# Two-layer decoder trunk on one core: first queries ahead of the first spread, attention interleaved eight steps later

## The chip, the core and the metric

The kernel runs on one core of one Trainium2 chip. The metric is the device time of one execution in microseconds (us). The core's engines work in parallel, each through its own queue in order: TensorE (PE in the profile, matmuls), VectorE (DVE), ScalarE (ACT), GpSimd (POOL) and SyncE (SP), which issues most of the DMAs. Sums of matmuls stand in PSUM, which has eight banks of 128x512 f32; everything else on the chip stands in SBUF.

## What is computed

Two layers on a sequence of 1024 tokens with 1024 channels. The first mixes by differential attention in 12 heads (two softmax maps for each head, the second weighted and subtracted), the second by causal pooling over windows. Both add a cross-attention over 256 memory tokens and a gate:

```
proj = rms_norm(h) @ W_in            # u (queries, keys, values), q_mem, gate
q, k = apply_rotary(q), apply_rotary(k)
s = q @ k.T * scale, causal          # 12 heads x 2 maps, 64 wide
p = softmax(s);  w = p[0] - lam * p[1]
o = rms_norm(w @ v) * (1 - lambda_init)
y = concat(o, memory_attention(q_mem)) * silu(gate)
h = h + y @ W_out
```

All matmuls keep f32 precision: each operand is split into a rounded part and a rest (`wh`, `wl` for weights, `hh`, `hl` for hidden values), and a product is three matmuls, lines 125 to 127.

## The kernel before

**Steps.** The whole projection work of the attention is a stream of small steps (`run_jobs`, line 168). A step is one of the 8 parts of a projection of one half of the sequence (512 tokens): three matmuls of 128x512. A projection has half 1 (tokens 512 to 1023) first and then half 0, 16 steps, and behind the last step of a half its evacuation is emitted (`query_evac`, `key_evac`, `value_evac`, `gate_evac`). The jobs are, in order, the values of head 0, then for each further head h its queries, its keys, the gate of head h-1 and its values, 64 steps for a head. `step(n)` takes n steps, `step_to(n)` steps up to a count n.

**Order.** TensorE's order is that in which the code emits; `attention_layer` (line 1334) writes it by hand. The other engines' queues are ordered by the compiler's scheduler, and each of them runs its queue strictly in sequence.

**Prologue** (line 337). x is loaded and scaled, the keys and queries of head 0 are projected for both halves outside the stream, and their evacuations are held back until the half's row scale is known. That scale comes from `row_means` (TensorE, `ms_h`, line 250), a Newton iteration on DVE (`rsxh`, `rsuh`, `rsyh`, lines 224 to 241) and `spread`: matmuls that copy the scale to all partitions (`bc_h`, line 530), an ACT copy to `rsb`, and on DVE the products of the rotation tables with it (lines 372 and 373). Then the held evacuations run: for a query or key, ACT copies four blocks of 32 partitions (`rot`, line 763), DVE and POOL multiply by the rotation tables (lines 764, 767) and add (768), and ACT and DVE split the result (`qa` and `qlo`, lines 783 to 785; `kb`, 802 and 803).

**Attention.** Head h's scores are made in blocks of 128 queries, i = 0 to 7. `scores` (line 834) emits the matmuls of both maps, adds the mask and takes the least on DVE (856), with two steps of the stream behind each set; then ACT takes two exponentials, one for each map (865). `combine` (871) takes the reciprocal (875) and the scaling (876) on DVE, the second map's product on POOL (877) and the sum on DVE (880). The weights are used in ten groups (p, jj): `turn_weights` (884) transposes them on TensorE (`wt`, 902) and splits them, `apply_weights` (911) multiplies them by the values into `o`. Group k+1 is turned before group k is applied. Blocks 6, 7 and 4 of a head are scored ahead of its first group, blocks 2, 5 and 3 during groups 0, 1 and 2, and block 5 is first needed when group 4 (`wt` of p = 2) is turned. The last line of the loop, `self.step_to(60 + 64 * h + per_step * (g + 1))`, keeps the stream at 6.4 steps a group, 4.0 in the last head, where no queries, keys and values follow. `hooks` are the norms of finished outputs (`attend_post`, 929): a Newton iteration on 128x128 numbers on DVE (`rsya`, `rsua`) and a trip through DRAM. `turns` are transposes of values.

**Weights.** Each projection's weights are loaded by SP and split: ACT rounds them (`wh`, line 115), POOL subtracts (`wl`, line 118).

## Time and profile before

| | us |
|---|---|
| median of 3 runs | 1843.71 |
| lowest and highest | 1839.75, 1844.18 |
| the profiled execution | 1845.75 |
| its span, first to last instruction | 1844.0 |
| TensorE busy in it | 1742.3 (94%) |
| VectorE, ScalarE, GpSimd busy | 1351.8, 950.4, 658.8 |

The mean granted clock of TensorE is 0.98. The attention of head 0 begins at 86 us, and its ten groups take some 67 us a head; the first spread is at 40 us, the second at 50.7. A row of a timeline gives the start, the duration, the engine, the line, the operation, output<-inputs by the program's names without their numbers, and in brackets how long the engine had been idle and what released it. A row of a list of waits gives the total, the number and the longest.

### The profile page before, as it was taken

What the parts mean: (1) busy time and instruction counts of PE and PEld (TensorE: products, weight loads), DVE (VectorE), ACT (ScalarE), POOL (GpSimd) and SP (SyncE); (2) the same over time, 40 slices, a digit from 0 to 9 for tenths busy, and PEclk for the clock granted to TensorE, in tenths of its full rate; (3) what the DMA queues carried; (4) which work ended last, traced back from release to release, by engine and by line L of the source; (5) the groups of instructions that cost most, each with busy time, mean ns of one, the idle gap of its engine ahead of it and who ended that gap; (6) DMA issues with size and microseconds to landing.
All of it is one profiled execution on the core that took longest, in us unless ns stands there. A gap on an engine that the chain in (4) does not pass through costs nothing.

```text
span 1844.0 us, 24841 instructions
## 1 busy us (share of the span) xinstructions
PE 1742.3 (94%) x8478; PEld 1447.5 (79%) x8478; DVE 1351.8 (73%) x2705; ACT 950.4 (52%) x1764; POOL 658.8 (36%) x563
## 2 busy tenths in 40 slices
PE   6899999999999999999999998997999999979997
PEld 4778888888888888888787886875788777768886
DVE  7778888788888889886657768678876767754513
ACT  6667667567657657743246546454543332324422
POOL 4334344344444434343241243300133433413452
PEclk8999999999999999999999999998999999989998
DMA  5011111111111111011463777642312121156542
GB/s 185 23 35 47 46 46 58 46 35 58 47 46 47 47 52 52 35 64 64 155 211 110 267 263 260 218 175 91 106 61 89 63 80 67 54 177 194 172 151 95
DMA packets 81679, 188.68 MB, mean 102 GB/s; under 512 B 9200, under 2 KB 17104, under 8 KB 81552
## 3 DMA queue, kind: packets, MB, share of 16 engines
q1 hardware_dynamic: 79296, 183.08, 29.6%
q10 hardware_dynamic: 2160, 3.75, 0.6%
q8 instruction: 67, 1.10, 0.3%
q14 instruction: 60, 0.49, 0.1%
q0 software_dynamic: 96, 0.26, 0.0%
HBM read 155.29 MB, written 31.77 MB: 101 GB/s over the span
## 4 chain that ended last, share of the span: by engine, by line
PE 69%; DVE 17%; ACT 6%; DMA 5%; issue 3%; POOL 0%; SPq 0%; DVEq 0%; ACTq 0%; POOLq 0%
PE s L851 4%; PE o L925 3%; PE ob L127 3%; PE ob L125 3%; PE ob L126 3%; PE ga L125 3%; PE ga L126 3%; PE ga L127 3%; PE v L125 2%; PE v L127 2%; PE v L126 2%; PE wt L902 2%; DMA zf<-z 2%; ACT rotq L763 2%; PE q L125 2%
## 5 line engine op out<-in xcount | busy, mean ns | idle before, releaser
L865 ACT ACTIVATE e<-e,st 128x640 f32<-128x640 f32 (+4 forms) x192 | 148.2, 773 | 111.7 <-DVE st L856 110.5
L118 POOL TENSOR_TENSOR wl_o<-wf_o,wh_o 128x384 fp32r<-128x384 f32 x64 | 100.1, 1563 | 237.4 <-ACT wh_o L115 193.3
L877 POOL TENSOR_SCALAR e<-e,st 128x640 f32<-128x640 f32 (+4 forms) x96 | 76.3, 795 | 198.5 <-DVE st L876 115.2
L118 DVE TENSOR_TENSOR wl_o<-wf_o,wh_o 128x640 fp32r<-128x640 f32 x64 | 60.7, 948 | 107.7 <-ACT wh_o L115 98.7
L1575 DVE TENSOR_TENSOR zr<-zf,zr 128x512 fp32r<-128x512 f32 x132 | 108.2, 841 | 38.0 <-ACT zr L1574 37.6
L115 ACT CAST wh_o<-wf_o 128x1024 fp32r<-128x1024 f32 x64 | 67.2, 1050 | 117.0 <-PE ob L126 65.7
L905 ACT CAST wth<-wt 128x512 fp32r<-128x512 f32 (+2 forms) x168 | 72.5, 431 | 105.3 <-PE wt L902 74.0
L1574 ACT CAST zr<-zf 128x512 fp32r<-128x512 f32 x132 | 80.7, 619 | 83.6 <-DMA zf<-z 59.8
L856 DVE CUSTOM_DVE_ANT_0 e<-s,mask 128x512 f32<-128x512 f32 (+2 forms) x192 | 109.5, 581 | 10.5 <-PE s L851 8.9
L125 PE MATMUL ga<-hh,wh_ga 128*128 128x512 f32 x256 | 104.9, 410 | 3.8 <-DVE mqf L620 3.8
L127 PE MATMUL ob<-zr,wl_o 128*128 128x512 f32 x256 | 100.9, 394 | 6.1 <-DVE wl_o L118 6.1
L126 PE MATMUL ga<-hl,wh_ga 128*128 128x512 f32 x256 | 101.6, 397 | 0.0
L127 PE MATMUL ga<-hh,wl_ga 128*128 128x512 f32 x256 | 101.5, 396 | 0.0
L851 PE MATMUL s<-kb,qa 128*128 128x512 f32 (+2 forms) x288 | 98.4, 349 | 2.9 <-DVE kb L803 2.9
L126 PE MATMUL ob<-zr,wh_o 128*128 128x512 f32 x256 | 100.7, 393 | 0.4 <-DVE zr L1575 0.4
L125 PE MATMUL ob<-zr,wh_o 128*128 128x512 f32 x256 | 100.9, 394 | 0.0
L851 PE MATMUL s<-kb,qlo 128*128 128x512 f32 (+2 forms) x288 | 98.3, 349 | 0.0
L906 DVE TENSOR_TENSOR wtl<-wt,wth 128x512 fp32r<-128x512 f32 (+2 forms) x168 | 82.8, 493 | 7.8 <-ACT wth L905 6.6
L125 PE MATMUL k<-hh,wh_k 128*128 128x512 f32 x192 | 79.1, 412 | 9.1 <-ACT wh_k L115 9.1
L880 DVE SCALAR_TENSOR_TENSOR e<-e,st,e 128x640 f32<-128x640 f32 (+4 forms) x96 | 77.9, 811 | 9.7 <-POOL e L877 9.0
L902 PE MATMUL wt<-cst,e 128*128 128x128 f32 x432 | 69.2, 274 | 13.9 <-DVE e L880 11.4
L125 PE MATMUL v<-hh,wh_v 128*128 128x512 f32 x192 | 79.7, 415 | 0.0
(1225 smaller groups left out, 5653.2 us busy)
## 6 DMA issues: line engine op xcount, KB each, us to landing
zf<-z SPq DMA_DIRECT2D x132, 256.0 KB, 4.1
wf_o<-in_w_out SPq DMA_DIRECT2D x64, 512.0 KB, 3.6
wf_ga<-in_w_in SPq DMA_DIRECT2D x16, 512.0 KB
wf_q<-in_w_in SPq DMA_DIRECT2D x12, 512.0 KB, 3.2
wf_v<-in_w_in SPq DMA_DIRECT2D x12, 512.0 KB, 4.1
z<-rs SPq DMA_DIRECT2D x24, 256.0 KB, 3.3
z<-z SPq DMA_DIRECT2D x24, 256.0 KB, 2.0
wf_k<-in_w_in SPq DMA_DIRECT2D x11, 512.0 KB, 3.2
```

Source lines behind the costliest of these rows:

```text
L118: eng.tensor_tensor(wl[:, c], wf[:, c], wh[:, c].bitcast(F32), op=ALU.subtract)
L125: nc.tensor.matmul(out, sh, mh, start=first, stop=False, skip_group_check=more)
L126: nc.tensor.matmul(out, sh, ml, start=False, stop=False, skip_group_check=more)
L127: nc.tensor.matmul(out, sl, mh, start=False, stop=last, skip_group_check=more)
L851: nc.tensor.matmul(sc[m][:, w], q[half][part][:, m, qs], k[kh][:, m, w], start=(part == 0), stop=(part == 1),)
L856: nc.vector.tensor_tensor_reduce(out=es[m][:, lo:hi], in0=sc[m][:, : hi - lo], in1=self.mask[:, S - n + lo : S - n + hi], scale=1.0, scala ...
L865: nc.scalar.activation(es[m][:, :n], es[m][:, :n], AF.Exp, bias=least[m], scale=-1.0, accum_out=st[:, 2, m : m + 1],)
L880: nc.vector.scalar_tensor_tensor(es[0][:, :n], es[0][:, :n], st[:, 3, 0:1], es[1][:, :n], op0=ALU.mult, op1=ALU.add)
L902: nc.tensor.transpose(t[:, c : c + P], w[b][:, j * P : (j + 1) * P], self.ident)
L906: nc.vector.tensor_tensor(wl[:, lo:hi], t[:, lo:hi], wh[:, lo:hi].bitcast(F32), op=ALU.subtract)
L1574: nc.scalar.copy(z[:, 0, :], zf)
L1575: nc.vector.tensor_tensor(z[:, 1, :], zf, z[:, 0, :].bitcast(F32), op=ALU.subtract)
```

## The change

In the prologue the queries of half 0 are projected before the first spread, in place of behind it. The second spread comes when 8 steps of the stream, the values of head 0 for half 1, have been taken. Blocks 6, 7 and 4 of head 0 are scored later in the stream, both turns of head 0's values come before them, and the groups' counts start at 68, not 60; the last head's share is 32 steps, not 40.

```diff
 project(1, 0, self.pj)
+project(0, 0, self.pj)
 spread(1)
 self.row_means(pool, sums[0], 0)
-project(0, 0, self.pj)
-spread(0)
 self.lambda_full(pool)
 self.count = 4 * KT
+self.step(KT)
+spread(0)
...
-            self.step_to(44)
+            self.step_to(46)
+            self.run_hooks()
+            self.step_to(52)
+            self.run_hooks()
             score_block(0, 6)
             self.step(3)
             score_block(0, 7)
-            self.step_to(57)
+            self.step_to(65)
             score_block(0, 4)
-            self.step_to(56)
-            self.run_hooks()
-            self.step_to(58)
-            self.run_hooks()
-            self.step_to(60)
+            self.step_to(BEGIN)
...
-                per_step = (64.0 if h + 1 < NH else 40.0) / len(order)
+                per_step = (64.0 if h + 1 < NH else 100.0 - BEGIN) / len(order)
...
-                self.step_to(60 + 64 * h + per_step * (g + 1))
+                self.step_to(BEGIN + 64 * h + per_step * (g + 1))
```

`BEGIN` is 68. The instructions are the same; their order on the engines is not, and the rows below show it at three places. In them a name carries its indices: `e550` is block 5 of head 5 in its first map, `e551` in its second, `qa60` the queries of head 6 for half 0, `rotk61` the rotated keys of head 6 for half 1.

ScalarE's queue in head 5, around the exponentials of block 5, before:

```order
L784 CAST qa60_4408<-fq60_4400 64x512
L783 CAST qa60_4408<-fq60_4400 64x512
L784 CAST qa60_4408<-fq60_4400 64x512
L865 ACTIVATE e550_4453,st55_4452<-e550_4453,st55_4452 128x768
L865 ACTIVATE e551_4454,st55_4452<-e551_4454,st55_4452 128x768
L763 ACTIVATE rotk61_4517<-k61_4427 32x512 x4
L905 CAST wth533_4542<-wt533_4541 128x256
L865 ACTIVATE e530_4557,st53_4556<-e530_4557,st53_4556 128x512
```

and after:

```order
L804 CAST kb61_4461<-fk61_4453 64x512 x2
L785 CAST qa60_4359<-fq60_4351 64x512
L786 CAST qa60_4359<-fq60_4351 64x512
L785 CAST qa60_4359<-fq60_4351 64x512
L786 CAST qa60_4359<-fq60_4351 64x512
L867 ACTIVATE e550_4492,st55_4491<-e550_4492,st55_4491 128x768
L116 CAST wh_v6_4572<-wf_v6_4570 128x1024
L765 ACTIVATE rotk60_4556<-k60_4472 32x512 x4
L867 ACTIVATE e551_4493,st55_4491<-e551_4493,st55_4491 128x768
L907 CAST wth533_4587<-wt533_4586 128x256
```

Before, the two exponentials stand next to each other, ahead of the copies of a key half (`rotk61`). After, that key half is already done, its splits (`kb61`) stand ahead of the query casts, and the weight cast `wh_v6` and the copies of the other key half (`rotk60`) stand between the two exponentials. Heads 1 to 10 have the same order.

GpSimd's queue in head 5, around the product of block 5, before:

```order
L877 TENSOR_SCALAR e521_4384<-e521_4384,st52_4382 128x384
L894 MEMSET wth533_4542 128x128
L895 MEMSET wtl533_4543 128x128
L877 TENSOR_SCALAR e551_4454<-e551_4454,st55_4452 128x768
L767 TENSOR_TENSOR rotk61_4517<-rotk61_4517,trig_tab_184 128x512
L877 TENSOR_SCALAR e531_4558<-e531_4558,st53_4556 128x512
L118 TENSOR_TENSOR wl_v6_4623<-wf_v6_4620,wh_v6_4622 128x1024
L767 TENSOR_TENSOR rotk60_4606<-rotk60_4606,trig_tab_184 128x512
```

and after:

```order
L769 TENSOR_TENSOR rotk61_4452<-rotk61_4452,trig_tab_184 128x512
L879 TENSOR_SCALAR e521_4428<-e521_4428,st52_4426 128x384
L896 MEMSET wth533_4587 128x128
L897 MEMSET wtl533_4588 128x128
L119 TENSOR_TENSOR wl_v6_4573<-wf_v6_4570,wh_v6_4572 128x1024
L769 TENSOR_TENSOR rotk60_4556<-rotk60_4556,trig_tab_184 128x512
L879 TENSOR_SCALAR e551_4493<-e551_4493,st55_4491 128x768
```

The weight subtraction `wl_v6` and the rotation of `rotk60` stood behind the product `e551`, and now stand ahead of it.

VectorE's queue in the prologue, around the last Newton steps for half 0, which the second spread reads (`rsyh`), before:

```order
L240 SCALAR_TENSOR_TENSOR rsuh_509<-rsuh_509,rsyh_508 128x4
L241 SCALAR_TENSOR_TENSOR rsyh_508<-rsuh_509,rsyh_508 128x4
L372 TENSOR_TENSOR trig_tab_184<-trig_tab_184,rsb_175 128x512
L239 TENSOR_TENSOR rsuh_509<-rsxh_506,rsyh_508 128x4
L373 SCALAR_TENSOR_TENSOR trig_tab_184<-trig_tab_184,cst_72,rsb_175 128x512
L764 SCALAR_TENSOR_TENSOR fk01_472<-k01_310,trig_tab_184 128x512
L764 SCALAR_TENSOR_TENSOR fq01_486<-q01_413,trig_tab_184 128x512
L240 SCALAR_TENSOR_TENSOR rsuh_509<-rsuh_509,rsyh_508 128x4
L241 SCALAR_TENSOR_TENSOR rsyh_508<-rsuh_509,rsyh_508 128x4
L768 TENSOR_TENSOR fk01_472<-fk01_472,rotk01_471 128x512
L768 TENSOR_TENSOR fq01_486<-fq01_486,rotq01_485 128x512
```

and after:

```order
L241 SCALAR_TENSOR_TENSOR rsuh_534<-rsuh_534,rsyh_533 128x4
L805 TENSOR_TENSOR kb01_505<-fk01_497,kb01_505 64x512 x2
L242 SCALAR_TENSOR_TENSOR rsyh_533<-rsuh_534,rsyh_533 128x4
L819 TENSOR_TENSOR vf01_592<-v01_567,rsb_175 128x512
L787 TENSOR_TENSOR qlo0_185<-fq01_511,qa01_519 64x512
L240 TENSOR_TENSOR rsuh_534<-rsxh_531,rsyh_533 128x4
L787 TENSOR_TENSOR qlo0_185<-fq01_511,qa01_519 64x512
L241 SCALAR_TENSOR_TENSOR rsuh_534<-rsuh_534,rsyh_533 128x4
L242 SCALAR_TENSOR_TENSOR rsyh_533<-rsuh_534,rsyh_533 128x4
L373 TENSOR_TENSOR trig_tab_184<-trig_tab_184,rsb_175 128x512
L374 SCALAR_TENSOR_TENSOR trig_tab_184<-trig_tab_184,cst_72,rsb_175 128x512
```

Before, the products of the tables, one product for the keys and one for the queries stand among the last four Newton steps. After, the evacuation of the keys up to their splits (`kb01`), that of the values (`vf01`) and the query splits (`qlo0`) stand ahead of the last three.

## The prediction

> **What bounds the kernel now.** The page has TensorE (PE) busy for 94% of the span. I read nine heads of the attention by windows first, then the list of TensorE's waits, then the timelines of the start and of one head. The sum of nine windows of 67 us each (200 to 803 us, heads 2 to 10):

> ```profile
> sum 603.00, PE 595.28 PEld 504.06 DVE 514.41 ACT 396.54 POOL 258.03; mean PE 66.14 PEld 56.01 DVE 57.16 ACT 44.06 POOL 28.67
> ```

> TensorE is busy for 595.28 of 603.00 us there, at a granted clock of 1.00 in every one of the nine. It is the bound of the attention, and what it loses is 7.7 us, under 0.9 us a head. Who it waits for, over the whole run (total, times, longest):

> ```profile
> PE wt L902 <- DVE e L880: 11.4, 11, 2.7
> PE bc_h L530 <- DVE rsyh L241: 6.9, 2, 4.6
> PE s L851 <- DVE kb L803: 2.9, 1, 2.9
> PE wt L902 <- DVE vl L827: 2.4, 1, 2.4
> PE o L925 <- DVE og L938: 0.4, 1, 0.4
> ```

> The first row is the one wait that each head has. Its eleven times are heads 0 to 10, the longest is head 0's, so the other ten average (11.4 - 2.7) / 10 = 0.87 us. The other rows, apart from the last, lie in the first 90 us. In order of time, with the last matmul group in front of the first wait:

> ```profile
> 34.89 0.39 PE L126 MATMUL k<-hl,wh_k 128*128 128x512 f32 x1
> 35.12 0.39 PE L127 MATMUL k<-hh,wl_k 128*128 128x512 f32 x1
> 40.15 2.06 PE L530 MATMUL bc_h<-cst,rsyh 128*128 128x128 f32 x8 [4.64 <-DVE rsyh L241]
> 50.72 1.05 PE L530 MATMUL bc_h<-cst,rsyh 128*128 128x128 f32 x8
> 62.92 0.50 PE L851 MATMUL s<-kb,qa 128*128 128x512 f32 x1 [2.95 <-DVE kb L803]
> 86.31 1.25 PE L902 MATMUL wt<-cst,e 128*128 128x128 f32 x8 [2.44 <-DVE vl L827]
> 107.39 0.55 PE L902 MATMUL wt<-cst,e 128*128 128x128 f32 x3 [2.72 <-DVE e L880]
> ```

> The waits of the start are 4.64 us for the first spread, 2.95 for the first scores, 2.44 for the first weight transposes and 2.72 for those of group 4, 12.75 us in all. A wait has a second price, the granted clock. In these windows behind the four waits it is the third number from the right:

> ```profile
> 40.00:47.00 7.00, 6.85 (x24) 6.18 (x25) 3.24 (x17) 2.07 (x3) 0.07 (x1) 0.51 0.84 206
> 63.00:67.50 4.50, 4.50 (x13) 3.34 (x14) 3.78 (x8) 2.48 (x4) 0.00 (x0) 0.62 0.00 0
> 84.00:90.00 6.00, 3.69 (x21) 3.18 (x22) 5.66 (x11) 4.92 (x10) 1.27 (x1) 1.00 0.00 0
> 108.00:112.00 4.00, 4.00 (x15) 3.41 (x14) 2.75 (x5) 3.88 (x6) 2.92 (x2) 0.57 0.00 0
> ```

> Behind the 4.64 us wait the clock is 0.51 for 7 us, behind 2.95 it is 0.62 for 4.5 us, behind 2.72 it is 0.57 for 4 us; behind 2.44 it stays at 1.00. Lost: 7 x 0.49 = 3.4, 4.5 x 0.38 = 1.7 and 4 x 0.43 = 1.7 us, 6.8 us together. So the start offers at most 12.75 + 6.8 = 19.6 us.

> **The change at the start.** The 24 matmuls of the first half's queries now stand ahead of the spread that is waited for. The timeline's row at 34.89 is followed at 35.12 by the last of the keys', 0.227 us apart, so 24 take 5.4 us, and the 4.64 us wait goes: the value that it waited for landed at 40.10. That DVE step is itself a sign of something that returns below:

> ```profile
> 37.80 2.30 DVE L241 SCALAR_TENSOR_TENSOR rsyh<-rsuh,rsyh 128x4 f32<-128x4 f32 x1
> ```

> ```profile
> 37.36 2.71 POOL L118 TENSOR_TENSOR wl_v<-wf_v,wh_v 128x1024 fp32r<-128x1024 f32 x1 [6.72 <-ACT wh_v L115]
> 47.05 1.30 POOL L767 TENSOR_TENSOR rotk<-rotk,trig_tab 128x512 f32<-128x512 f32 x1 [6.97 <-DVE trig_tab L373]
> 51.82 2.40 POOL L118 TENSOR_TENSOR wl_q<-wf_q,wh_q 128x1024 fp32r<-128x1024 f32 x1 [2.23 <-ACT wh_q L115]
> ```

> A Newton step on 128x4 numbers took 2.30 us, until 40.10, because POOL's subtraction ran from 37.36 to 40.07: a DVE operation with both inputs in SBUF stood still until POOL had ended. After the first spread (from 40.8, copied by ACT at about 42.4) POOL's next subtraction, 2.40 us by the row at 51.82, now stands ahead of the rotations, so DVE's first product of the rotation tables, two SBUF inputs, is held to about 44.3, and the Newton steps of the second half stand behind it. They also stand, in DVE's queue, behind both halves of a key split, the first value evacuation and two query splits (the third piece of order above). The second spread comes when TensorE has done the first 24 value matmuls, at about 40.8 + 1.9 + 5.4 = 48 (1.9 for the first spread, 1.05 by the row at 50.72, and nearly as much for the means). If DVE has by then only the value's evacuation, two splits and small steps left, it is late by 2.4 us (0.68 each); if the two rotation products on POOL, 1.30 us each by the row at 47.05, hold it as well, it is done near 54, late by 6.0. I take 6.0, because these products are released by the held table and nothing else runs on DVE in between.

> The 2.95 us wait for the first scores goes. The keys let the scores begin at 62.92, 12.2 us behind the second spread at 50.72, so after a spread at 54 at about 66. The scores are due behind the spread (2), 13 steps of 0.69 us (9.0), two turns (0.7) and a drop of the clock (1.7), at 67.4. The first transposes wait for block 7's exponentials; between its two maps ACT's queue now has a weight cast and four rotation copies (3.44 us by rows below), which I take for a wait of 3.5 us in place of 2.44 (bounds: nothing, 6). Head 0's later wait grows like that of the other heads, to about 4.5. New waits 6.0 + 3.5 + 4.5 = 14.0 against 12.75, three clock drops against three: +1.3 us, which I take as 0. The lower bound is 2.4 + 0 + 2.4 + 2.7 = 7.5 with one drop fewer, so -7; the upper one +5.

> **The change in each head.** This is where the sum is made. Attention runs 8 steps behind where it ran, relative to the projections, in all heads, so other evacuations fall between block 5's scores and its weights, which the 0.87 us wait is for. TensorE in head 5: the first matmul behind block 5's last scores, and the transpose that waits:

> ```profile
> 433.32 0.40 PE L125 MATMUL k<-hh,wh_k 128*128 128x512 f32 x1
> 444.40 0.55 PE L902 MATMUL wt<-cst,e 128*128 128x128 f32 x3 [0.74 <-DVE e L880]
> ```

> The transpose was due at 444.40 - 0.74 = 443.66, that is 10.34 us behind 433.32; the number of matmuls between the two is the same after the change. What ACT does in that time, and the DVE addition that gives the first of these casts its input:

> ```profile
> 434.92 0.62 ACT L783 CAST qa<-fq 64x512 fp32r<-64x512 f32 x1 [1.41 <-PE k L127]
> 437.48 0.94 ACT L865 ACTIVATE e<-e,st 128x768 f32<-128x768 f32 x1
> 438.42 0.92 ACT L865 ACTIVATE e<-e,st 128x768 f32<-128x768 f32 x1
> 439.24 0.19 ACT L865 ACTIVATION_READ_ACCUMULATOR e<-e,st 128x1 f32 x1
> 439.45 2.39 ACT L763 ACTIVATE rotk<-k 32x512 f32<-32x512 f32 x4
> 446.81 1.05 ACT L115 CAST wh_v<-wf_v 128x1024 fp32r<-128x1024 f32 x1
> ```

> ```profile
> 434.14 0.68 DVE L768 TENSOR_TENSOR fq<-fq,rotq 128x512 f32<-128x512 f32 x1
> ```

> Now: four query casts from 434.92 to 437.48, block 5's two exponentials, the accumulator read at 439.43 (6.11 us behind 433.32), and only then the rotation copies of a key half (2.39). After: the casts can start at 0.1, since the addition, which today ends at 434.82, is done earlier (the row names a matmul for their wait; if that is true, they start at 1.6 as today, and all that follows is 1.5 us later), so the first exponential ends at 0.1 + 2.56 + 0.94 = 3.6. Then come a weight cast of 1.05 and the four copies of 2.39, moved between the two exponentials in ACT's queue in every head from 1 to 10. The second ends at 3.6 + 3.44 + 1.01 = 8.06, 1.95 us later than now.

> Behind it follow DVE's reciprocal and scaling, POOL's product and DVE's sum:

> ```profile
> 428.08 1.41 DVE L785 TENSOR_TENSOR qlo<-fq,qa 64x512 fp32r<-64x512 f32 x1
> 439.20 0.29 DVE L239 TENSOR_TENSOR rsua<-rsx,rsya 128x128 f32<-128x128 f32 x1
> 440.81 0.68 DVE L856 CUSTOM_DVE_ANT_0 e<-s,mask 128x512 f32<-128x512 f32 x1
> 442.04 0.68 DVE L764 SCALAR_TENSOR_TENSOR fk<-k,trig_tab 128x512 f32<-128x512 f32 x1
> 443.34 1.00 DVE L880 SCALAR_TENSOR_TENSOR e<-e,st,e 128x768 f32<-128x768 f32 x1
> ```

> ```profile
> 427.63 1.30 POOL L940 TENSOR_TENSOR sql<-sq,sqh 128x512 fp32r<-128x512 f32 x1 [1.39 <-ACT sqh L939]
> 429.81 2.40 POOL L118 TENSOR_TENSOR wl_ga<-wf_ga,wh_ga 128x1024 fp32r<-128x1024 f32 x1 [0.88 <-ACT wh_ga L115]
> 441.06 0.91 POOL L877 TENSOR_SCALAR e<-e,st 128x768 f32<-128x768 f32 x1 [3.29 <-DVE st L876]
> 441.94 1.33 POOL L767 TENSOR_TENSOR rotk<-rotk,trig_tab 128x512 f32<-128x512 f32 x1
> ```

> Today this takes from 439.43 to 444.34, 4.91 us. With the same 4.91 the sum ends at 12.97, and the transpose waits 12.97 + 0.06 - 10.34 = 2.7 us: that is the lower bound. For the upper one: POOL's queue, too, now has a weight subtraction and a key rotation ahead of block 5's product, 2.40 and 1.33 us, from about 4.7 to 8.5. The first row of DVE shows what that does: a split of normally 0.69 us took 1.41, since POOL's operation of 427.63 ended at 428.93. In the same stretch DVE's queue has the Newton steps of the previous head's norm (0.29 each, two SBUF inputs), which today run while POOL is idle. If they are held to 8.5, there follow on DVE to the end of the scaling 3.4 us (two reductions and a rotation product at 0.6, six steps of 0.1 to 0.3, a split), the key's addition 0.6, POOL's product 0.91, small steps 0.95 and the sum 1.00, so it ends at 15.4 and the wait is 5.1 us, or 6.6 if the casts start at 1.6. I take 4.3, nearer 5.1 than 2.7, because the key's copies end (7.05) only when the weight subtraction does (7.1), so POOL goes from one to the other. That is 3.4 us more a head, for ten heads 34 us. Each such wait is longer than the 2.72 us behind which the clock fell, so 1.7 us a head comes on top, 17 us.

> [...]

> **The last head.** It has 34 steps of projection in place of 40. The only wait in it today is the last row of the list of waits, 0.4 us, and the six steps (4.1 us) are work that was done earlier, not new work. I take 0; if all of them were cover, +4. Nothing behind the attention is moved but a few evacuations, and the DMAs that load weights come in the same sequence.

> **Sum.** 0 + 34 + 17 = 51 us. On the profiled execution, 1845.75 us (span 1844.0 and 1.75 outside it), that is 1896.8; it stands 2.04 us above the median of the runs shown, so on that median 1843.71 + 51 = 1895.

> **The rivals.** *The short wait.* POOL's two operations hold DVE little, and the wait is the 2.7 us of the lower bound: 18 us more in ten heads, with the clock dropping in none to all of them 0 to 17 us: 1862 to 1879. For it speaks that Newton steps may slip through where POOL changes from one operation to the next; against it, that each such change lets one through. *Faster.* The chain behind the second exponential shrinks from 4.91 to 3.15 us (10.34 + 0.87 - 8.06), where the wait in each head is what it is today; then only the start counts, 1843.71 - 7 = 1837. Every 0.1 us above 3.15 takes back 1 us of that. For it speaks that DVE lost time in 4.91 to other heads' work; against it, that more of that work stands ahead after the change. *No change.* The chain takes about 3.7 us, the ten heads lose 5, and the start gives as much: 1844. *More.* A wait of 6.6 us, that is 57 us in ten heads, a drop of 3.4 us behind each, 34, and 5 at the start: 1940.

> **How the numbers follow.** A measurement of this kernel tells 0.3%, 5.5 us, from no change. My forecast has 0.53, the short wait 0.20, more 0.04, no change 0.10, faster 0.13: 4.91 us to 3.15 is a distance that the interleaving of other heads' work on DVE could make up by itself. Slower is thus 0.77, same 0.10, faster 0.13. The range goes from 1844, so that it holds the short wait whole, to 1915, which is 20 us above the forecast: waits of 5.1 us, 8 more in ten heads, with drops of 2.9. It leaves out about 2 in 10, most of them faster.

> **What would show it.** In the profile after: no wait of the first spread, a wait of 2 to 6 us at the second; each head of 200 to 800 us about 72 us long, not 67; the wait of the weight transposes for DVE's sum at 40 us or more in place of 11.4, with one drop of the clock a head; ACT's second exponential of block 5 about 3.4 us behind the first. If that wait stays at 11 us, the step is wrong that says the two exponentials' distance reaches TensorE. [...] If the heads are 67 us and the time is still longer, it is the start that I read wrongly.

## The result, and the profile after

| | us | runs |
|---|---|---|
| before, median | 1844.18 (1839.75 to 1848.20) | 5 |
| after, median | 1925.08 (1920.20 to 1925.57) | 5 |
| ratio after to before | 1.0426, 95% interval 1.0407 to 1.0445 | |
| forecast | 1895, range 1844 to 1915 | |

The kernel is 80.9 us slower. The direction was forecast; the size was not, and it lies outside the range. The profiled execution after has a span of 1923.3 us, 79.3 more than the one of before. Who TensorE waits for, after:

```profile
PE wt L904 <- DVE e L882: 50.6, 13, 4.2
PE s L853 <- DVE st L858: 16.9, 11, 2.5
```

The first row was 11.4 us before. The second row, scores that wait for `st`, that is for the evacuation that frees their PSUM bank, did not stand in the list of before at all. In order of time, one head from one wait of the weight transposes to the next:

```profile
467.11 0.39 PE L853 MATMUL s<-kb,qa 128*128 128x256 f32 x1 [1.49 <-DVE st L858]
481.99 0.90 PE L904 MATMUL wt<-cst,e 128*128 128x128 f32 x3 [4.21 <-DVE e L882]
556.83 0.90 PE L904 MATMUL wt<-cst,e 128*128 128x128 f32 x3 [4.21 <-DVE e L882]
```

Each head now has a wait of 4.21 us (0.71 to 1.06 before) and, 14.9 us ahead of it, one of about 1.5 us at the second set of block 5's scores. The head lasts 74.84 us here (74.2 on average), against 67.2 on average before. The granted clock is the third number from the right in these windows, 9 us behind each of the two longer waits:

```profile
481.99:490.99 9.00, 9.00 (x34) 7.61 (x35) 5.06 (x9) 1.53 (x3) 0.51 (x1) 0.67 0.12 29
556.83:565.83 9.00, 9.00 (x42) 7.67 (x43) 6.17 (x14) 2.01 (x4) 0.51 (x1) 0.85 0.10 31
```

The clock loses 9 x 0.33 = 3.0 us behind the first and 9 x 0.15 = 1.4 us behind the second, which follows a wait of the same length. Over the ten heads it is 22.6 us.

ScalarE and GpSimd in that head, and VectorE from the Newton steps to block 5's sum:

```profile
470.32 0.94 ACT L867 ACTIVATE e<-e,st 128x768 f32<-128x768 f32 x1
471.26 1.03 ACT L116 CAST wh_v<-wf_v 128x1024 fp32r<-128x1024 f32 x1
472.32 2.39 ACT L765 ACTIVATE rotk<-k 32x512 f32<-32x512 f32 x4
474.74 0.94 ACT L867 ACTIVATE e<-e,st 128x768 f32<-128x768 f32 x1
```

```profile
472.38 2.40 POOL L119 TENSOR_TENSOR wl_v<-wf_v,wh_v 128x1024 fp32r<-128x1024 f32 x1 [0.56 <-ACT wh_v L116]
474.85 1.30 POOL L769 TENSOR_TENSOR rotk<-rotk,trig_tab 128x512 f32<-128x512 f32 x1
479.48 1.32 POOL L879 TENSOR_SCALAR e<-e,st 128x768 f32<-128x768 f32 x1 [3.33 <-ACT wth L907]
```

```profile
473.21 1.65 DVE L235 TENSOR_SCALAR rsya<-rsx 128x128 int32<-128x128 int32 x1
474.90 1.40 DVE L240 TENSOR_TENSOR rsua<-rsx,rsya 128x128 f32<-128x128 f32 x1
480.93 1.00 DVE L882 SCALAR_TENSOR_TENSOR e<-e,st,e 128x768 f32<-128x768 f32 x1
```

The weight cast and the four key copies stand between the two exponentials, as the order had shown: the second begins 3.5 us after the first has ended. GpSimd's subtraction for the value weights runs from 472.38 to 474.78 and its key product from 474.85 to 476.15; in that time two Newton steps on VectorE take 1.65 and 1.40 us, where before the same two took 0.23 and 0.29 (438.93 and 439.20). Everything behind them in VectorE's queue, the scaling of block 5 among it, comes later; the sum ends at 481.93, and TensorE goes on 0.06 us later.

The other wait has a similar picture. What VectorE does ahead of block 5's evacuation, and GpSimd beside it:

```profile
463.10 0.69 DVE L766 SCALAR_TENSOR_TENSOR fk<-k,trig_tab 128x512 f32<-128x512 f32 x1 [1.31 <-ACT rotk L765]
464.04 1.11 DVE L878 TENSOR_TENSOR st<-st,coef 128x2 f32<-128x2 f32 x1
466.37 0.68 DVE L858 CUSTOM_DVE_ANT_0 e<-s,mask 128x512 f32<-128x512 f32 x1
463.84 1.29 POOL L769 TENSOR_TENSOR rotk<-rotk,trig_tab 128x512 f32<-128x512 f32 x1
```

VectorE's queue has the first product of the next head's key in front of block 5's scores. It stands idle for 1.31 us until ScalarE's copies of that key are done; then a multiplication of 128x2 numbers takes 1.11 us (0.15 at 440.74 before), because GpSimd's key product holds it until 465.13. Block 5's first scores were in their banks at about 464.0, and are taken out from 466.37 on.

The start, where the old wait was 4.64 us and has become 0.67, and the second spread:

```profile
39.93 1.16 PE L532 MATMUL bc_h<-cst,rsyh 128*128 128x128 f32 x8 [0.67 <-DVE rsyh L242]
54.59 2.04 PE L532 MATMUL bc_h<-cst,rsyh 128*128 128x128 f32 x8 [7.14 <-DVE rsyh L242]
```

**Where the 79.3 us are.** Cut at the waiting transposes of group 4 of head 0 (107.39 before, 110.47 after), the same of head 10 (779.41 and 852.21), and the first gate matmul behind the attention (903.79 and 975.55). The attention is 8 steps further on in the projections at the first two cuts, which are 24 matmuls of 0.227 us, 5.4 us of work that is not new.

| stretch | before | after | more | without the 5.4 us moved |
|---|---|---|---|---|
| start and head 0 | 107.39 | 110.47 | +3.1 | -2.3 |
| ten heads | 672.02 | 741.74 | +69.7 | +69.7 |
| last head | 124.38 | 123.34 | -1.0 | +4.4 |
| behind the attention | 940.2 | 947.8 | +7.5 | +7.5 |

In the ten heads, the waits of the weight transposes are 42.1 us in place of 8.7 (+33.4), those of the scores 15.6 in place of none, and of the clock's loss 20.9 us fall into the stretch, against 1.7 before (+19.2): 68.2 of 69.7 us.

### The profile page after: what moved, and what is told of

The parts are those of the page before. It is cut to its first block, busy times and chain, and to the rows that moved or that the text cites. A ratio compares the mean times of both kernels' runs of the same rounds, so it can differ in the third digit from the quotient of the medians.

```text
span 1923.3 us, 24778 instructions
## 1 busy us (share of the span) xinstructions
PE 1771.3 (92%) x8478; PEld 1470.0 (76%) x8478; DVE 1378.8 (72%) x2705; ACT 953.9 (50%) x1764; POOL 653.3 (34%) x563
## 4 chain that ended last, share of the span: by engine, by line
PE 55%; DVE 27%; ACT 7%; DMA 5%; issue 3%; POOL 1%; SPq 1%; DVEq 0%; ACTq 0%; POOLq 0%
DVE e L858 3%; PE ob L128 3%; PE ob L127 3%; PE ob L126 3%; ACT e L867 3%; PE o L927 2%; PE s L853 2%; PE v L126 2%; PE v L128 2%; PE v L127 2%; PE ga L126 2%; PE ga L127 2%; PE ga L128 2%; DVE rsua L241 2%; PE wt L904 1%
## 5 line engine op out<-in xcount | busy, mean ns | idle before, releaser
L879 POOL TENSOR_SCALAR e<-e,st 128x640 f32<-128x640 f32 (+4 forms) x96 | 82.4, 859 | 200.5 <-DVE st L878 112.9
L116 ACT CAST wh_o<-wf_o 128x1024 fp32r<-128x1024 f32 x64 | 67.2, 1050 | 117.7 <-PE ob L127 68.3
L853 PE MATMUL s<-kb,qa 128*128 128x512 f32 (+2 forms) x288 | 99.8, 352 | 16.9 <-DVE st L858 16.9
L882 DVE SCALAR_TENSOR_TENSOR e<-e,st,e 128x640 f32<-128x640 f32 (+4 forms) x96 | 101.6, 1058 | 17.7 <-POOL e L879 17.3
L126 PE MATMUL ga<-hh,wh_ga 128*128 128x512 f32 x256 | 111.7, 436 | 1.9 <-DVE mqf L622 1.9
L127 PE MATMUL ga<-hl,wh_ga 128*128 128x512 f32 x256 | 106.3, 415 | 0.0
L128 PE MATMUL ga<-hh,wl_ga 128*128 128x512 f32 x256 | 105.8, 413 | 0.0
L904 PEld LDWEIGHTS wt<-cst,e 128*128 128x128 f32 x432 | 54.3, 145 | 64.5 <-DVE e L882 55.1
L127 PE MATMUL ob<-zr,wh_o 128*128 128x512 f32 x256 | 100.6, 393 | 0.0
L126 PE MATMUL ob<-zr,wh_o 128*128 128x512 f32 x256 | 100.5, 393 | 0.0
L126 PE MATMUL k<-hh,wh_k 128*128 128x512 f32 x192 | 79.4, 414 | 8.3 <-ACT wh_k L116 8.3
```

Of the source, the lines that this page charges most:

```text
L126: nc.tensor.matmul(out, sh, mh, start=first, stop=False, skip_group_check=more)
L127: nc.tensor.matmul(out, sh, ml, start=False, stop=False, skip_group_check=more)
L128: nc.tensor.matmul(out, sl, mh, start=False, stop=last, skip_group_check=more)
L853: nc.tensor.matmul(sc[m][:, w], q[half][part][:, m, qs], k[kh][:, m, w], start=(part == 0), stop=(part == 1),)
L879: nc.gpsimd.tensor_scalar(es[1][:, :n], es[1][:, :n], st[:, 3, 1:2], 1.0, op0=ALU.mult, op1=ALU.mult)
L882: nc.vector.scalar_tensor_tensor(es[0][:, :n], es[0][:, :n], st[:, 3, 0:1], es[1][:, :n], op0=ALU.mult, op1=ALU.add)
```

## The experiments

Each ran on one chip beside the kernel before, whose medians there were 1845 to 1848 us. The first theory, A, was the prediction's: the loss is made in each head, by the work put between block 5's exponentials.

**The change cut in two: new_start, new_heads.** In the first the attention's lines are those of before, in the second the prologue's.

```diff
-            self.step_to(46)
+            self.step_to(44)
...
-BEGIN = 68
+BEGIN = 60
```

```diff
-        project(0, 0, self.pj)
         spread(1)
         self.row_means(pool, sums[0], 0)
+        project(0, 0, self.pj)
+        spread(0)
...
-        self.step(KT)
-        spread(0)
```

> The changed order of the start (first-half queries before the first spread, 8 steps of values before the second spread), with the attention at its old places (first scores at step 44, groups from step 60, last head over 40 steps). Theory A (the loss is made in every head, by a weight cast and four key copies that stand between the two exponentials of block 5): the heads are back at 67.1 us and the wait of the weight transposes at 0.9 us; only the start is left, where the second spread waits 7.1 us: 1844 + 4 = 1848 us, 1842 to 1856. Theory B (the start is the source, and the heads lose because they are fed late by it): 1900 us or more.

Measured: 1847.4 us, ratio 1.0012 (1.0001 to 1.0022).

> The old order of the start, with the attention at its new places (first scores at step 52, groups from step 68, last head over 32 steps). Theory A: the same work stands between block 5's exponentials as in the changed kernel, so ten heads lose 69.7 us (74.2 in place of 67.2) and the end 6.5: 1844 + 76 = 1920 us, 1912 to 1928, with a wait of 4.2 us a head. Theory B: 1844 to 1852 us.

Measured: 1924.3 us, ratio 1.0418 (1.0396 to 1.0440). The waits of the two, new_start first:

```profile
PE wt L904 <- DVE e L882: 11.3, 11, 1.8
```

```profile
PE wt L903 <- DVE e L881: 51.9, 13, 4.3
PE s L852 <- DVE st L857: 14.9, 10, 2.3
```

The start costs about 2 us and the new place of the attention all the rest. It is not fed late by the start: with the old start the same two waits are there, 51.9 and 14.9 us.

**Other places: begin70, begin72, begin64, begin66.** If the work between the exponentials makes the loss, places at which nothing stands there must be fast.

```diff
-BEGIN = 68
+BEGIN = 70
```

> The changed kernel with groups from step 70 in place of 68, two steps later still (last head over 30 steps). On ScalarE nothing then stands between the two exponentials of block 5, while the four copies of a key half still stand between those of block 2. Theory A: the wait of the weight transposes falls from 4.2 us to about 1 (0.5 to 2.7) and the clock drops behind it go (2.3 us a head), the 1.5 us wait of block 5's scores stays: 1925 - 10 x (3.3 + 2.3) = 1869 us, 1858 to 1882. Theory C (it is the shift itself, later work against the same evacuations, that costs): as slow or slower, 1925 to 1945 us.

Measured: 1958.0 us, ratio 1.0596 (1.0572 to 1.0620).

> The changed kernel with groups from step 72 (last head over 28 steps). On ScalarE nothing stands between the exponentials of blocks 5 and 2. Theory A: both the 4.2 us wait and the 1.5 us wait go, about 1925 - 10 x 7 = 1855 us, 1846 to 1868; what stays is the start's 3 us and the last head's 6 us or more. Theory C: 1930 to 1960 us.

Measured: 1952.8 us, ratio 1.0574 (1.0557 to 1.0591). Theory A fell here by 90 to 100 us each time. C has begin72 in its range, but begin70 is above its own, and is the slower of the two. In begin70 block 5's exponentials do follow each other, and the wait is the longest of all:

```profile
494.80 0.90 PE L904 MATMUL wt<-cst,e 128*128 128x128 f32 x3 [6.28 <-DVE e L882]
484.21 0.94 ACT L867 ACTIVATE e<-e,st 128x768 f32<-128x768 f32 x1
485.14 0.92 ACT L867 ACTIVATE e<-e,st 128x768 f32<-128x768 f32 x1
481.84 2.48 POOL L119 TENSOR_TENSOR wl_v<-wf_v,wh_v 128x1024 fp32r<-128x1024 f32 x1 [6.03 <-ACT wh_v L116]
483.30 1.39 DVE L235 TENSOR_SCALAR rsya<-rsx 128x128 int32<-128x128 int32 x1
484.72 1.29 DVE L240 TENSOR_TENSOR rsua<-rsx,rsya 128x128 f32<-128x128 f32 x1
```

The weight cast and the copies now stand ahead of both exponentials, and GpSimd's two operations again hold Newton steps (1.39 and 1.29 us). I formed A2: the evacuation of the second key half and the value split must not stand ahead of the end of block 5's chain.

> The changed kernel with groups from step 64 in place of 68 (last head over 36 steps). The value cast and the second key half's copies stand behind block 5's exponentials, between those of block 3. Theory A2: block 5's chain ends as early as before the change, wait 0.5 to 2 us without a clock drop, no wait of block 5's scores: 1848 to 1868 us. Theory C: half of the loss, 1880 to 1895 us.

Measured: 1932.7 us, ratio 1.0463 (1.0447 to 1.0480).

> The changed kernel with groups from step 66 (last head over 34 steps). Only the two casts of the first key half (1.26 us) stand between block 5's exponentials; value cast and second key half come behind them. Theory A2: the wait is 1.3 us longer than before the change or a little more, 2 to 3 us, at the edge of a clock drop: 1858 to 1888 us. Theory C: 1900 to 1912 us.

Measured: 1931.1 us, ratio 1.0458 (1.0437 to 1.0478). A2 failed as well, and so did C: four steps later than before cost as much as eight. In begin64 the exponentials are early (the second ends at 402.85), and the sum is late all the same:

```profile
413.26 0.90 PE L904 MATMUL wt<-cst,e 128*128 128x128 f32 x3 [4.91 <-DVE e L882]
407.67 2.40 POOL L119 TENSOR_TENSOR wl_v<-wf_v,wh_v 128x1024 fp32r<-128x1024 f32 x1 [0.35 <-ACT wh_v L116]
410.15 1.26 POOL L769 TENSOR_TENSOR rotk<-rotk,trig_tab 128x512 f32<-128x512 f32 x1
407.89 2.33 DVE L241 SCALAR_TENSOR_TENSOR rsua<-rsua,rsya 128x128 f32<-128x128 f32 x1
410.25 1.71 DVE L805 TENSOR_TENSOR kb<-fk,kb 64x512 fp32r<-64x512 f32 x1
```

A Newton step of 0.29 us takes 2.33, until GpSimd's subtraction is over; the next key split, 0.69 us, takes 1.71 beside GpSimd's key product; block 5's sum follows at 412.20. What the slow places have in common is not ScalarE's order, but that these two operations of GpSimd fall between block 5's scores and its sum. That is theory D. It is not the whole: in begin72 the two run from 480.59 to 484.35 beside evacuations from PSUM, which keep their 0.69 us, and hold no step of VectorE ahead of block 5's sum. The wait there is 3.43 us even so; the scaling comes 4.6 us after the second exponential has been read out, behind two evacuations of scores, three operations of 0.69 us of a key's and a gate's evacuation and four Newton steps in VectorE's queue.

**The exponentials brought together: pair_kept, late_key.** Two ways to put ScalarE's order right at the place of the change, both by an order that the data enforce.

In pair_kept, and likewise in front of the copies of the second key half:

```diff
+            if name[0] == "v" and self.kept and name == f"v{self.kept[0] + 1}":
+                nc.scalar.copy(wh[:, lo : lo + 1], self.kept[1][:, 2, 1:2])
             nc.scalar.copy(wh[:, lo : lo + n], wf[:, lo : lo + n])
```

In late_key, with the evacuation of the first key half called behind block 5's scores:

```diff
+        if self.kept and half == 1 and name == f"k{self.kept[0] + 1}":
+            nc.scalar.copy(rot[:, 0:1], self.kept[1][:, 0, 1:2])
```

> The changed kernel with one thing undone: the next head's value cast and the copies of its second key half are made to wait for the second exponential of block 5 (a 128x1 copy of that block's sums into their output, overwritten at once), so that on ScalarE the two exponentials follow each other, and on GpSimd the value subtraction and that key's product come after them. Theory A2 (the loss is made by the evacuation of the next head's second key half and the value split standing ahead of the end of block 5's chain, whether between its exponentials or in front of both): the wait of the weight transposes falls from 4.2 us to under 1.5 and the clock drops behind it go, the scores' wait of 1.5 us stays: 1925 - 10 x (3 to 3.4 + 2.3) = 1868 us, 1852 to 1885. Theory C (any later place of the attention costs, about 10 us a step): 1910 to 1930 us.

Measured: 1913.5 us, ratio 1.0365 (1.0346 to 1.0383).

> The changed kernel, with the evacuation of the next head's first key half made to wait for block 5's first maxima (a 128x1 copy on ScalarE, overwritten at once). On VectorE block 5's score evacuations then stand ahead of that key's products, and on ScalarE its two exponentials follow each other; the value subtraction still comes right behind them. Theory D: the scores' wait of 1.5 us a head goes (-15 us), the wait of the weight transposes stays at 3 to 5 us, since GpSimd's subtraction still falls into block 5's chain: 1905 to 1920 us. Theory A (ScalarE's distance between the two exponentials makes the wait): both waits go, 1850 to 1872 us.

Measured: 1946.3 us, ratio 1.0543 (1.0523 to 1.0563). The time of pair_kept lies in C's range, which begin64 and begin66 rule out; A2's wait of under 1.5 us did not come, it is 2.12. The head of pair_kept, and behind it that of late_key:

```profile
474.38 0.55 PE L910 MATMUL wt<-cst,e 128*128 128x128 f32 x3 [2.12 <-DVE e L888]
471.08 2.42 POOL L121 TENSOR_TENSOR wl_v<-wf_v,wh_v 128x1024 fp32r<-128x1024 f32 x1
471.20 3.13 DVE L888 SCALAR_TENSOR_TENSOR e<-e,st,e 128x768 f32<-128x768 f32 x1
```

```profile
419.04 0.90 PE L915 MATMUL wt<-cst,e 128*128 128x128 f32 x3 [5.92 <-DVE e L893]
410.00 2.41 POOL L119 TENSOR_TENSOR wl_v<-wf_v,wh_v 128x1024 fp32r<-128x1024 f32 x1 [2.83 <-ACT wh_v L116]
410.42 2.00 DVE L889 TENSOR_TENSOR st<-st,coef 128x2 f32<-128x2 f32 x1
```

In pair_kept the value subtraction moved back with its cast, and lands on block 5's sum itself: 3.13 us where 1.00 is normal. A new wait of 2.11 us at another block's scores came with it. In late_key the multiplication that scales block 5, 0.15 us, takes 2.00. The two exponentials follow each other in both; the waits are 2.12 and 5.92 us. The scores' wait went down in late_key (9.7 us in all, from 16.9), but the key's work, moved behind, made the sum later, and a wait of 1.0 us a head came at the gate matmuls, so both forecasts were missed upwards, D's by 26 us.

**The hold taken away, and put in: no_hold, begin70_no_hold, before_hold.**

In no_hold, and with BEGIN = 70 in begin70_no_hold:

```diff
+            if name[0] == "v" and name[1:].isdigit():
+                for _ in range(4):
+                    nc.gpsimd.memset(wl[:, lo : lo + n].bitcast(F32), 0.0)
+                continue
```

In before_hold, on the kernel before:

```diff
+                if i == 5:
+                    nc.gpsimd.tensor_copy(dull[:, 0:1], st[:, 2, 0:1])
+                    nc.gpsimd.tensor_tensor(dull, self.cosr, self.sinr, op=ALU.subtract)
```

> The changed kernel with GpSimd's subtraction of the value weights (both inputs in SBUF, 2.4 us) replaced by four memsets of the same tile, which read nothing; the low part of the value weights is left out by it, in all heads. Orders on ScalarE and VectorE stay as they are. If GpSimd's subtraction holds VectorE's Newton steps (1.65 and 1.40 us in place of 0.23 and 0.29) and that holds block 5's scaling, the wait falls by 1.3 to 1.7 us, the 1.65 and 1.40 fall to about 0.25 and 0.3: 1886 to 1908 us. If the hold is only slack in front of ScalarE's late second exponential: 1918 to 1930 us.

Measured: 1882.9 us, ratio 1.0191 (1.0174 to 1.0208).

```profile
460.11 0.55 PE L908 MATMUL wt<-cst,e 128*128 128x128 f32 x3 [1.82 <-DVE e L886]
452.93 1.96 POOL L119 MEMSET wl_v<- 128x1024 f32 x2
453.71 0.25 DVE L239 TENSOR_SCALAR rsya<-rsx 128x128 int32<-128x128 int32 x1
454.00 0.29 DVE L244 TENSOR_TENSOR rsua<-rsx,rsya 128x128 f32<-128x128 f32 x1
```

ScalarE's order is that of the changed kernel, with cast and copies between the exponentials. Beside memsets of about 1 us each the Newton steps take 0.25 and 0.29 us, the wait falls from 4.21 to 1.82, the clock drops behind it in none of the ten heads (it drops once, behind a scores' wait of 2.19 us), and 42 of the 81 us are gone, a little more than forecast, because nearly all of the clock's loss in the heads went too. The kernel is still 35 us above the one before, with 16.1 us of waits at scores left.

> The kernel with groups from step 70 (6.28 us of wait a head), with the value weights' subtraction on GpSimd replaced by four memsets (the low part of the value weights is left out in all heads). Theory D: the Newton steps of 1.39 and 1.29 us fall to about 0.25 and 0.3, the wait by 2 to 2.8 us to 3.5 to 4.3, with shorter clock drops: 1958 - 25 to 50 = 1908 to 1933 us. If the hold has no part in what is lost at this place: 1950 to 1960 us.

Measured: 1938.5 us, ratio 1.0500 (1.0480 to 1.0520), 20 us less than begin70, with a wait of 4.2 in place of 6.3 us. The wait came as forecast; the clock kept dropping behind 4.2 us, and the time is 5.5 us above the forecast. At this place the hold is worth 20 of the 113 us that are lost against before, so most of the loss there is something else.

> The kernel before, with one operation more in each head: a subtraction of the two rotation tables on GpSimd (128x1024, both inputs in SBUF, about 2.4 us, its result used by nobody), released by the sums of block 5's first exponential. Orders of all other instructions stay but for one neighbouring pair on VectorE. Theory D (what costs is a GpSimd operation of that length standing in the time in which VectorE brings block 5's sum about): VectorE's Newton steps of 0.23 to 0.29 us are held to its end, the sum ends 1.6 to 2.2 us later, the wait of the weight transposes grows from 0.9 to 2.5 to 3 us a head, at the edge of a clock drop: 1846 + 17 to 42 = 1863 to 1888 us. If the hold has only slack in front of it: 1842 to 1850 us.

Measured: 1890.2 us, ratio 1.0236 (1.0212 to 1.0260).

```profile
463.94 0.55 PE L902 MATMUL wt<-cst,e 128*128 128x128 f32 x3 [3.31 <-DVE e L880]
456.17 2.40 POOL L1364 TENSOR_TENSOR dull<-trig_tab 128x1024 f32<-128x1024 f32 x1
456.34 2.38 DVE L239 TENSOR_TENSOR rsua<-rsx,rsya 128x128 f32<-128x128 f32 x1
```

This is the converse. In the old kernel, with nothing else moved but one neighbouring pair on VectorE, one GpSimd operation whose result nobody reads (and a 128x1 copy that releases it) makes a Newton step of 0.29 us last 2.38, the waits grow from 0.7 to 1.1 us to 3.2 to 3.5, and 44 us are lost. The waits are 0.2 to 0.5 us and the time 2 us above what D gave. GpSimd itself is free again at 458.57, before VectorE takes block 5's reciprocal at 458.96, so its work for block 5 was not kept back; it is the hold of VectorE that TensorE pays for.

**Both together: pair_no_hold.** The edits of pair_kept and no_hold.

> Both changes at once on the changed kernel: value cast and second key half wait for block 5's second exponential (as in pair_kept), and four memsets stand for GpSimd's subtraction of the value weights (as in no_hold; the low part of the value weights is left out in all heads). Theory D2 (the 4.2 us are two parts: about 2.4 from GpSimd's hold, about 1.8 from ScalarE's distance between the exponentials): the block's sum, 3.13 us in pair_kept because it is itself held, takes 1.0 to 1.7, the wait of the weight transposes is 0 to 0.9; the scores' waits (1.5 and 2.1 us a head) stay: 1913 - 10 x 1.2 to 2.1 = 1892 to 1902 us, and no clock drops behind that wait. If the distance on ScalarE plays no part once the hold is gone, the wait is 1.8 as in no_hold.

Measured: 1897.7 us, ratio 1.0277 (1.0257 to 1.0297).

```profile
467.09 0.55 PE L914 MATMUL wt<-cst,e 128*128 128x128 f32 x3 [0.36 <-DVE e L892]
464.93 2.10 DVE L892 SCALAR_TENSOR_TENSOR e<-e,st,e 128x768 f32<-128x768 f32 x1
```

The wait is 0.36 us, so the 4.21 us divide: 2.4 go with GpSimd's subtraction (4.21 to 1.82), 1.5 with the cast and the copies between the exponentials (1.82 to 0.36), and the 0.36 us left are less than the wait before. The shares depend on the order: with pair_kept first, which also moves the subtraction, they are 2.1 (4.21 to 2.12) and 1.8. The sum takes 2.10, longer than forecast, beside GpSimd's key product. The time is still 52 us above before, with 36.5 us of waits at scores, the new one of pair_kept among them.

**Two ways to do better: v_on_dve, before_late_k.** Neither did. In v_on_dve:

```diff
+        if name[0] == "v" and name[1:].isdigit():
+            dve = n
```

In before_late_k, on the kernel before:

```diff
+        if self.kept and half == 1 and name == f"k{self.kept[0] + 1}":
+            nc.scalar.copy(rot[:, 0:1], self.kept[1][:, 0:1])
```

> The changed kernel with the low part of the value weights subtracted by VectorE in place of GpSimd (nothing is left out; the 128x1024 subtraction, about 1.5 us by the 0.94 us that 640 columns take, stands in VectorE's queue ahead of the Newton steps). Theory D2: the Newton steps of 1.65 and 1.40 us fall to about 0.25 and 0.3 (-2.5 us), the subtraction itself adds 1.5: wait 3.0 to 3.4 us a head, 1925 - 10 x 0.8 to 1.2, with the clock drops the same or up to 10 us shorter: 1903 to 1917 us. If GpSimd's hold is not it: 1935 to 1945 us, since VectorE has 1.5 us more to do.

Measured: 1922.2 us, ratio 1.0398 (1.0372 to 1.0424).

```profile
480.19 0.90 PE L906 MATMUL wt<-cst,e 128*128 128x128 f32 x3 [4.00 <-DVE e L884]
471.62 1.22 DVE L121 TENSOR_TENSOR wl_v<-wf_v,wh_v 128x1024 fp32r<-128x1024 f32 x1
476.98 0.70 DVE L880 TENSOR_TENSOR st<-st,coef 128x2 f32<-128x2 f32 x1
```

The forecast was missed, though GpSimd's subtraction is gone and the subtraction on VectorE took only 1.22 us: VectorE's order changed with it, a key split and the next block's scaling came ahead of the sum, and that scaling, 0.15 us, took 0.70 beside GpSimd's product for block 5. The wait is 4.0 us. VectorE is on the path here. Whether it matters that it is held or busy, this run can't tell, since its order changed as well.

> The kernel before, with the evacuation of the next head's first key half made to wait for block 5's sum (a 128x1 copy on ScalarE, overwritten at once), so that GpSimd's product for that key, which ends at 443.27 in the profile of before, just ahead of block 5's sum at 443.34, no longer stands in front of it. Theory D: the wait of 0.87 us a head falls to 0 to 0.4: 1845 - 5 to 9 = 1836 to 1840 us. If that key's work, moved behind, comes to stand in the chain of block 3: slower, 1850 to 1880 us.

Measured: 1866.1 us, ratio 1.0110 (1.0087 to 1.0133). The wait of 0.87 us a head is gone, as forecast; in its place the gate matmuls wait 2.1 us a head for the PSUM bank that the later key still occupies, which I had not thought of. No kernel here is faster than the one before.

## Why the prediction was wrong in size

Point by point, in its own steps.

- *The start, taken as 0.* Forecast waits 0, 6.0, none, 3.5 and 4.5 us, measured 0.67, 7.14, 1.29, 4.11 and 0.60: 13.8 in all, against 14.0. By new_start, in ten runs, it is worth +2 us; the -2.3 of the table is one execution against one. The total is right, in part by luck: head 0's later wait is 3.9 us shorter than forecast, and the other four are longer by 3.7 us together.
- *The wait in each head.* Forecast 4.3, measured 4.21; 34 us for ten heads, measured 33.4. From the matmul behind block 5's last scores (467.45) the first query cast comes at 0.3 (forecast 0.1), the second exponential is read out at 8.3 (8.06), GpSimd's two operations run from 4.9 to 8.7 (4.7 to 8.5), the sum ends at 14.5 (between 12.97 and 15.4). The mechanism is right; that the wait was met to 0.1 us is in part luck, by the next point.
- *What it is made of.* The lower bound said that without GpSimd's hold the wait would be 2.7; no_hold has 1.82. The 4.91 us that I took for the chain of before already had holds in them (rows of before, below): two Newton steps took 0.69 and 0.78 us where 0.29 is normal, 0.9 us together, which is the difference. So ScalarE's distance was made too large and the hold too small. I also told the order of ScalarE first; begin70, begin64 and late_key show that it need not be there for the wait to be as long or longer.
- *"1.7 us a head comes on top, 17 us".* Mis-sized: 22.6 us, since six of the ten drops last 6.83 us in place of 3.41 and cost 2.4 to 3.0 us.
- *What was not in the sum: a second wait.* "0 + 34 + 17 = 51 us" has one wait a head. The scores of block 5 wait as well, 1.3 to 2.5 us, 15.6 in ten heads. I followed VectorE's queue behind block 5's scores and not in front of them, where the first product of the next key now stands; the orders of ScalarE and GpSimd shown ahead of the prediction have that key half (`kb61`, `rotk61`) in front already. This is the step that failed, and the range failed with it: its upper end allowed for longer waits and deeper drops, but not for a second place. Without these 15.6 us the time would be 1909.5, inside the range.
- *The last head, 0 or +4.* The prediction counts 34 steps in place of 40; the edit leaves 32, so eight steps, 5.4 us, are moved. It is +4.4 without the moved work: a wait of 3.74 us for a sum, which head 11 didn't have before, with a drop of the clock.
- *Behind the attention nothing moves.* +7.5 us, of which the clock makes 6.9 (35.0 us lost against 28.1, added up over windows of 5 us), with waits of 57.2 us against 58.8. Runs of the kernel before differ by 8.4 us among themselves, and the same stretch is 943.1 us in new_start, with 32.9 lost; why the clock drops more often there stays open.

The rows of before, VectorE in head 5:

```profile
441.42 0.69 DVE L239 TENSOR_TENSOR rsua<-rsx,rsya 128x128 f32<-128x128 f32 x1
442.64 0.78 DVE L240 SCALAR_TENSOR_TENSOR rsua<-rsua,rsya 128x128 f32<-128x128 f32 x1
```

The sum with the measured terms: -2.3 + 33.4 + 15.6 + 19.2 + 1.5 (not assigned) + 4.4 + 7.5 = 79.3 us. Of the rivals, the short wait is what the kernel would be without GpSimd's hold (1883 us in no_hold, forecast 1862 to 1879).

What stays open besides the clock behind the attention: the scores' wait was read from the profile, and no run took it away by itself. Two runs bear it out: in begin66 the key's first product (469.31) stands behind block 5's first evacuations (468.10 and 468.70), and the ten heads have no wait at these scores, though others came; in late_key, which moves it behind them, the ten waits are 9.1 us in place of 15.6. Not followed up were the losses of begin72 (20.0 us of a wait for the value split among them).

## What to carry to other kernels

When a schedule is shifted by a few steps, look first at where GpSimd's long operations fall relative to the chain that the bound engine waits for: a change that moves no work onto that chain can still make its shortest steps on VectorE five to thirteen times as long (0.29 to 1.40 us after, 0.15 to 2.00 in late_key). List the moved instructions on every queue both behind and ahead of each product that is waited for, since a late consumer and a late evacuation in front of it are separate waits and separate terms of the sum. A measured chain taken over as a constant carries the holds of its old surroundings; price it from undisturbed durations and add the holds of the new ones.

## What the runs showed of the hardware

**Who holds VectorE.** Operations of VectorE that stood until GpSimd's subtraction of two SBUF tiles ended: a Newton step with two inputs in SBUF (0.29 to 2.38 us in before_hold), and also the integer operation on one 128x128 tile (0.23 to 1.65 us after). The products that take a query or key half out of PSUM (line 766) kept their length beside a GpSimd operation with two SBUF inputs: 0.69 us in all 23 cases after, 0.68 to 0.69 in the 21 beside no GpSimd operation. GpSimd's memsets held nothing (0.25 and 0.29 us in no_hold). Why the integer operation, with one input, is held as well, no run shows.

**When the clock drops.** Waits of about the same length in ten heads of a kernel, and the heads in which the clock fell in the 9 us behind:

| wait, us | kernel | heads with a drop | lost in a drop, us |
|---|---|---|---|
| 1.5 to 1.8 | no_hold | 0 of 10 | |
| 2.1 | pair_kept | 3 of 9 | 1.7 |
| 3.2 to 3.5 | before_hold | 8 of 10 | 1.5 to 2.8 |
| 4.2 | after | 10 of 10 | 1.4 to 3.0 |

```profile
461.57:464.98 3.41, 1.04 (x6) 0.95 (x7) 3.41 (x9) 0.69 (x3) 0.90 (x1) 1.00 0.00 0
464.98:468.39 3.41, 3.41 (x12) 2.93 (x11) 3.35 (x7) 3.33 (x6) 1.62 (x2) 0.50 0.03 7
533.25:536.66 3.41, 1.49 (x8) 1.31 (x9) 3.41 (x10) 1.12 (x3) 0.49 (x2) 1.00 0.00 0
```

In the first stretch TensorE is idle for 2.37 us, and the next one, the second row, is at 0.50. The wait of the third row is the longer one, 3.53 us, but it falls into two stretches with 1.6 and 1.9 us idle, and behind it the clock stays at 1.00 (1.00 over the 9 us from 535.17). With the traces of before and after cut in the same way from 100 to 950 us, each of the 13 full-clock stretches with 2.30 us or more of idle time is followed by a drop, none of the 466 with 1.91 us or less is, and none lies between. Outside this part of the two traces 6 of 20 drops follow less than 1.80 us; why stays open. No run varied the idle time within such a stretch alone, so that it is what decides is not shown.
